# Turning blocks as whole sheets in a two-layer encoder on one core

## The chip, the cores and the metric

The kernel runs on one core of a Trainium2 chip. TensorE (PE in the profile) multiplies matrices, VectorE (DVE) and ScalarE (ACT) work on elements, and SyncE (SP) issues transfers on its own queue; GpSimd (POOL) makes only a few constants. Operands lie in SBUF, products are summed in PSUM, weights come from HBM. The metric is the device time of one execution in microseconds (us), here as the median of several runs.

## The reference

Two layers of an encoder over 256 rows (tokens) of width D = 2048, and 256 rows of memory. Everything is float32.

```python
h = rmsnorm(x, g);  proj = h @ w_in[l]                 # 2048 x 7168
a_x, a_b, a_c, a_g, d_q, d_k, d_v, d_g, m_q, m_g = split(proj)
# A: gated convolution over rows, 6 groups of 128 columns
y_a = a_b * conv3(a_c * a_x) * silu(a_g)
# D: differential attention, 6 heads of two halves of 64, q and k normed per half
y_d = silu(d_g) * (1 - lam_init) * rmsnorm((softmax(q1 k1 + alibi) - lam * softmax(q2 k2 + alibi)) v)
# M: attention of 4 heads of 128 into the memory, queries and keys normed
mk, mv = split(rmsnorm(mem) @ w_mem_kv[l])
y_m = silu(m_g) * softmax(norm(m_q) norm(mk)) mv
x = x + concat(y_a, y_d, y_m) @ w_out[l]
```

## The kernel before, in words

**Products and chunks.** The 256 rows are two row tiles of 128 (`NT`), the 2048 columns 16 k-tiles of 128 (`KT`). To keep float32 accuracy, each operand is split into a high and a low half, and each product is three matmuls: high by high (L250), high by low (L251), low by high (L252), each 128x128 by 128x512. `block` computes 512 columns of a projection for both row tiles in two PSUM accumulators. It walks the k-tiles in **chunks** of two (`CK`): one load of 512 KB into one of four raw buffers (L219, SyncE's queue), one high half by ScalarE (L225; with the gain of a norm L229), one low half by VectorE (L226, L230), four buffers of each, and 12 matmuls, 2.72 us at the spacing of the profile. There are 320 chunks, numbered here from 0: 0 to 7 the memory keys of layer 0, 8 to 15 its values, 16 to 23 the keys of layer 1 (x is loaded meanwhile, L581, eight transfers), 24 to 31 its values, 32 to 175 layer 0, 176 to 319 layer 1. In a layer come the six blocks of group D, the two of M, the six of A and the output projection (chunks 144 to 175 and 288 to 319).

**Turns.** The stationary operand of a product has the contracted columns on the partitions: it is a turned block, `xT`, `yT` and `memT`, as high and low half for each k-tile (`split_T`: high by ScalarE at L206 or L209, low by VectorE). Before the change there are three ways to turn a block of 256 rows by 512 columns:

- `turn`, for the memory heads' keys and queries: eight TensorE transposes of 128x128 (L337), evacuated by ScalarE with the gain (L340).
- `turn32`, for group D's queries and keys, the convolution's gate and input, and columns 0 to 1023 of layer 1's x: 16 VectorE transposes (L352), each of four partition quarters into one of four, in squares of 32x32. The squares are put in place by the instruction's own input and output, so each has 32 partitions.
- `x_rows` with `rows_T`, for all of layer 0's x and columns 1024 to 2047 of layer 1's: four TensorE transposes for two k-tiles (L518).

**What sets the order.** Such work is written as generators in the queue `side`; `run_side` takes one step after each chunk, and `later` holds a generator back for some chunks. A scheduler then orders the instructions of each engine by its own estimate of times and by their priority; `keep_in_program_order` pins some. What stands on an engine's queue behind an instruction that waits, waits too. Loads, halves and side work of one engine share its queue.

**Sums of squares.** `normed` squares both accumulators of a block (L315, ScalarE), sums by group (L316) and multiplies by the inverse root (L325). `x_square` sums the squares of x (L548): eight calls, for four column blocks and two row tiles, written before layer 0's first block.

Of the kernel before, what the change touches and what calls it, by code (L numbers as in the profile page):

```python
# [14 lines left out]
ALU = mybir.AluOpType  # L15
# [19 lines left out]
PARTS = 8  # L35

# [7 lines left out]
def encoder(ctx: ExitStack, tc: tile.TileContext, x, mem, norm_g, w_in, conv_w, conv_b,  # L44
# [83 lines left out]
    kgain = const.tile([P, DEPTH], F32, name="kgain")  # L128
    neglam = const.tile([P, DEPTH], F32, name="neglam")
    lam_init = [0.8 - 0.6 * math.exp(-0.3 * l) for l in range(DEPTH)]  # L130

    def rest_of_constants():
# [33 lines left out]
    side = deque()  # L166
# [3 lines left out]
    def later(g, n):  # L170

        due[id(g)] = chunk[0] + n
        return g

    def run_side(n=1, now=None):
        chunk[0] += now is None
        for _ in range(n):
            g = next((g for g in side if now or due.get(id(g), 0) <= chunk[0]), None)
            if g is None:
                return  # L180
            side.remove(g)
            try:
                next(g)
                if len(side) >= 1:
                    side.insert(1, g)
                else:
                    side.append(g)
            except StopIteration:
                due.pop(id(g), None)

    def flush_side():
        while side:
            run_side(now=True)
# [9 lines left out]
    def split_T(dst, k, src, gain):  # L203

        if gain is None:
            in_order(nc.scalar.copy(dst[:, 0, k, :], src),  # L206
                     nc.vector.tensor_tensor(dst[:, 1, k, :], src, dst[:, 0, k, :].bitcast(F32), ALU.subtract))
        else:
            nc.scalar.activation(dst[:, 0, k, :], src, AF.Copy, scale=gain)  # L209
            nc.vector.scalar_tensor_tensor(dst[:, 1, k, :], src, gain, dst[:, 0, k, :].bitcast(F32),  # L210
                                           ALU.mult, ALU.subtract)
# [22 lines left out]
    def block(stat, w, cols, order, steps=1, gain=None, before=None, apart=0, acc=None, more=False):  # L234
# [28 lines left out]
        for c in range(0, n, CK):  # L263
# [7 lines left out]
            for j in range(CK):  # L271
                k = k0 + j
                hi, lo = parts[j]
# [35 lines left out]
    def normed(acc, gs, st, whole=False):  # L309
# [10 lines left out]
        res = []  # L320
        both = tmp.tile([P, NT, NB], F32, tag="e", name=nm("nat")) if whole else None
        for t in range(NT):
            nc.vector.tensor_scalar(r[:, t], r[:, t], col(st, R, t), None, ALU.mult)
            y = both[:, t] if whole else tmp.tile([P, NB], F32, tag="nat", name=nm("nat"), bufs=4)
            nc.vector.tensor_tensor(y.rearrange("p (g d) -> p g d", d=gs),  # L325
                                    acc[t].rearrange("p (g d) -> p g d", d=gs),
                                    r[:, t].unsqueeze(2).to_broadcast([P, ng, gs]), ALU.mult)
            res.append(y)
        return both if whole else res

    def turn(nat, dests):


        for t in range(NT):
            pt = ps_t.tile([P, NB], F32, tag="t", name=nm("pt"))
            for j in range(NB // P):
                nc.tensor.transpose(pt[:, j * P:(j + 1) * P], nat[t][:, j * P:(j + 1) * P], ident)  # L337
            at = 0
            for dst, h0, nh, gain in dests:
                nc.scalar.activation(dst[:, h0:h0 + nh, t * P:(t + 1) * P],  # L340
                                     pt[:, at * P:(at + nh) * P].rearrange("p (h q) -> p h q", h=nh),
                                     AF.Copy, scale=gain)
                at += nh
            yield

    def turn32(dst, src):

        n = src.shape[-1] // P
        B = 32
        for b in range(P // B):  # L350
            for a in range(P // B):
                tc.keep_in_program_order(nc.vector.transpose(  # L352
                    dst[b * B:(b + 1) * B, 0:n].rearrange("p j (t a c) -> p t j a c", a=P // B, c=B)[:, :, :, a, :],
                    src[a * B:(a + 1) * B].rearrange("p t (j b c) -> p t j b c", b=P // B, c=B)[:, :, :, b, :]))
            yield
# [46 lines left out]
    def qk_T(l, yT, k2, nat, q, k, tag):  # L402

        whole = keep.tile([P, NB // P, SEQ], F32, tag=tag, name=nm("qk"))
        yield from turn32(whole, nat)
        if q is not None:
            c0, h0, nh = q
            a = c0 // P
            for c in range(2):
# [3 lines left out]
                nc.scalar.copy(hi, src)  # L413
                nc.vector.tensor_tensor(yT[other, c, h0:h0 + nh, :], src, hi.bitcast(F32), ALU.subtract)
                yield
        if k is not None:
            c0, h0, nh = k
            a = c0 // P
            for c in range(2):
# [4 lines left out]
                nc.scalar.activation(hi, src, AF.Copy, scale=g)  # L424
                nc.scalar.activation(yT[other, c, CG + h0:CG + h0 + nh, :], src, AF.Copy, scale=g)
                for at, n, dst, d0 in ((0, min(nh, 4 - h0), yT, CG + DH + h0), (4 - h0, h0 + nh - 4, k2, 0)):
                    if n > 0:
                        lo = dst[own, c, d0:d0 + n, :]
                        nc.vector.scalar_tensor_tensor(lo, whole[own, a + at:a + at + n, :], g,  # L429
                                                       hi[:, at:at + n].bitcast(F32), ALU.mult, ALU.subtract)  # L430
                        nc.scalar.copy(dst[other, c, d0:d0 + n, :], lo)
# [332 lines left out]
```

## Time and profile before

| | |
|---|---|
| median of three runs | 955.16 us (954.63 to 956.37) |
| the profiled execution | 953.96 us |
| its span, first to last instruction | 952.2 us |
| TensorE busy | 943.5 us, 99% |
| VectorE, ScalarE busy | 718.9 us (76%), 513.1 us (54%) |
| granted TensorE clock, mean | 0.999 |
| moved by transfers | 175.21 MB in 103,523 packets |

A row of groups reads: line, engine, operation, output and inputs, shape, count, then busy time, mean ns of one, and the idle time of the engine just before, with what ended it. A row of the timeline reads: start, duration, engine, line, operation, count of like neighbours that it joins, and in brackets the idle time before it. A row of waits reads: who waits, for what, microseconds in all, times, longest. Matmuls overlap: each takes about 0.39 us, and the next begins 0.23 us after it.

### The profile page before, as it was taken

The page shows a single profiled execution, that of the slowest core. Times are in us where ns is not written, and L with a number is a line of the kernel's source. Part 1 is how long each engine was busy: PE and PEld are TensorE (multiplying, and loading weights), DVE is VectorE, ACT ScalarE, POOL GpSimd, SP SyncE. Part 2 cuts the span into 40 slices and gives each one's busy share as a digit, 9 for nine tenths or more (in the row PEclk, how much of TensorE's full clock was granted, in tenths as well). Part 3 has the DMA queues.
Part 4 walks back from the last instruction along what each step waited for, and adds up shares of the span by engine and source line. Part 5 has one row for each costly group of instructions (what it writes and reads, how often), then busy time and mean ns, then how long its engine had stood idle before and what let it go on. Part 6 is the DMA issues. An engine that isn't in the chain of part 4 may idle for free.

```text
span 952.2 us, 12481 instructions
## 1 busy us (share of the span) xinstructions
PE 943.5 (99%) x4370; PEld 778.7 (82%) x4370; DVE 718.9 (76%) x1408; ACT 513.1 (54%) x803; POOL 1.4 (0%) x8
## 2 busy tenths in 40 slices
PE   8999999999999999999999999999999999999998
PEld 6888788888888888888878888888888888888886
DVE  5766679996677788668798679995677787569752
ACT  5857645675456654443555445675455645444531
POOL 0000000000000000000000000000000000000000
PEclk9999999999999999999999999999999999999999
DMA  8786556557655556654646666556665555654672
GB/s 269 258 267 193 159 180 191 168 164 226 187 169 162 168 159 181 183 161 131 227 147 226 191 186 196 160 172 221 177 177 164 168 159 173 181 173 155 196 251 83
DMA packets 103523, 175.21 MB, mean 184 GB/s; under 512 B 6318, under 2 KB 29732, under 8 KB 103460
## 3 DMA queue, kind: packets, MB, share of 16 engines
q1 hardware_dynamic: 102116, 173.09, 59.2%
q10 hardware_dynamic: 1344, 1.33, 0.5%
q8 instruction: 34, 0.56, 0.2%
q14 instruction: 29, 0.24, 0.1%
HBM read 172.29 MB, written 2.10 MB: 183 GB/s over the span
## 4 chain that ended last, share of the span: by engine, by line
PE 86%; DVE 10%; issue 2%; ACT 1%; DMA 0%; ACTq 0%; DVEq 0%
PE acc L251 27%; PE acc L252 27%; PE acc L250 26%; DVE lo L226 3%; PE po L382 2%; DVE uT L352 2%; DVE qk L352 1%; PE ptT L375 1%; DVE xf L352 1%; PE pt L518 1%; PE s L488 1%; ACT hi L225 1%; DVE yT L429 0%; DMA raw<-in_w_mem_kv_dram 0%; PE py L367 0%
## 5 line engine op out<-in xcount | busy, mean ns | idle before, releaser
L226 DVE TENSOR_TENSOR lo<-raw,hi 128x1024 fp32r<-128x1024 f32 x288 | 350.3, 1222 | 148.8 <-ACT hi L225 146.8
L225 ACT CAST hi<-raw 128x1024 fp32r<-128x1024 f32 x288 | 301.5, 1051 | 283.5 <-PE acc L252 234.6
L251 PE MATMUL acc<-lo,xT 128*128 128x512 f32 x896 | 352.0, 393 | 0.1
L252 PE MATMUL acc<-hi,xT 128*128 128x512 f32 x896 | 348.6, 392 | 0.0
L250 PE MATMUL acc<-hi,xT 128*128 128x512 f32 x896 | 348.4, 394 | 0.1
L251 PEld LDWEIGHTS acc<-lo,xT 128*128 128x128 f32 x896 | 168.4, 188 | 35.0 <-DVE lo L226 1.5
L250 PEld LDWEIGHTS acc<-hi,xT 128*128 128x128 f32 x896 | 168.4, 188 | 34.6 <-ACT xT L209 0.6
L252 PEld LDWEIGHTS acc<-hi,xT 128*128 128x128 f32 x896 | 167.9, 188 | 33.6
L251 PE MATMUL acc<-lo,yT 128*128 128x512 f32 x256 | 99.8, 391 | 2.0 <-DVE lo L226 2.0
L252 PE MATMUL acc<-hi,yT 128*128 128x512 f32 x256 | 98.0, 389 | 0.0
L250 PE MATMUL acc<-hi,yT 128*128 128x512 f32 x256 | 95.1, 390 | 0.0
L251 PEld LDWEIGHTS acc<-lo,yT 128*128 128x128 f32 x256 | 48.1, 188 | 13.6 <-DVE lo L226 3.7
L230 DVE SCALAR_TENSOR_TENSOR lo<-raw,cva,hi 128x512 fp32r<-128x512 f32 x64 | 45.6, 747 | 17.2 <-ACT hi L229 17.0
L250 PEld LDWEIGHTS acc<-hi,yT 128*128 128x128 f32 x256 | 48.1, 188 | 9.9
L252 PEld LDWEIGHTS acc<-hi,yT 128*128 128x128 f32 x256 | 48.1, 188 | 9.8
L229 ACT ACTIVATE hi<-raw,cva 128x512 fp32r<-128x512 f32 x64 | 42.5, 716 | 19.6 <-PE acc L252 14.9
L252 PE MATMUL acc<-hi,memT 128*128 128x512 f32 x124 | 48.6, 392 | 0.0
L251 PE MATMUL acc<-lo,memT 128*128 128x512 f32 x124 | 48.4, 390 | 0.0
L250 PE MATMUL acc<-hi,memT 128*128 128x512 f32 x124 | 44.4, 395 | 0.1
L352 DVE STREAM_TRANSPOSE qk<-nat 32x256 f32<-32x256 f32 x96 | 41.8, 436 | 1.5
L251 PEld LDWEIGHTS acc<-lo,memT 128*128 128x128 f32 x124 | 23.3, 188 | 5.0
L252 PEld LDWEIGHTS acc<-hi,memT 128*128 128x128 f32 x124 | 23.3, 188 | 4.9
(153 smaller groups left out, 725.5 us busy)
## 6 DMA issues: line engine op xcount, KB each, us to landing
raw<-in_w_in_dram SPq DMA_DIRECT2D x192, 512.0 KB
raw<-in_w_out_dram SPq DMA_DIRECT2D x64, 512.0 KB
raw<-in_w_in_dram SPq DMA_DIRECT2D x64, 256.0 KB
raw<-in_w_mem_kv_dram SPq DMA_DIRECT2D x31, 512.0 KB
xs<-in_x_dram SPq DMA_DIRECT2D x8, 256.0 KB
xs<-in_mem_dram SPq DMA_DIRECT2D x7, 256.0 KB
out_dram<-xs SPq DMA_DIRECT2D x8, 128.0 KB
out_dram<-xs ACTq DMA_DIRECT2D x8, 128.0 KB
```

The costliest lines, as they stand in the source:

```text
L225: nc.scalar.copy(hi, raw)
L226: nc.vector.tensor_tensor(lo_, raw, hi.bitcast(F32), ALU.subtract)
L229: in_order(nc.scalar.activation(hi[:, j], raw[:, j], AF.Copy, scale=gains_of(j)), nc.vector.scalar_tensor_tensor(lo_[:, j], raw[:, j], gai ...
L230: nc.vector.scalar_tensor_tensor(lo_[:, j], raw[:, j], gains_of(j), hi[:, j].bitcast(F32), ALU.mult, ALU.subtract))
L250: nc.tensor.matmul(acc[t], sh, hi, start=first, stop=False)
L251: nc.tensor.matmul(acc[t], sh, lo, start=False, stop=False)
L252: nc.tensor.matmul(acc[t], sl, hi, start=False, stop=last)
L352: tc.keep_in_program_order(nc.vector.transpose(dst[b * B:(b + 1) * B, 0:n].rearrange("p j (t a c) -> p t j a c", a=P // B, c=B)[:, :, :, a ...
L375: nc.tensor.transpose(pt[:, k, i * P:(i + 1) * P], e[:, i, k * P:(k + 1) * P], ident)
L382: nc.tensor.matmul(po[:, i, :], eT[:, k, i * P:(i + 1) * P], v[:, k, h * P:(h + 1) * P], start=k == 0, stop=k == NT - 1)
L488: nc.tensor.matmul(s[:, i, :], qT[:, h, i * P:(i + 1) * P], kT[:, h, :], start=True, stop=True)
L518: nc.tensor.transpose(pt[:, j, t * P:(t + 1) * P], src(k + j, t), ident)
```

## The change

**Sheets.** A block to be turned is written by its makers (`normed`, the gate, the convolution's products) straight into a **sheet**: 128 partitions by 4 column quarters by n groups by 2 row tiles by 32 columns. One VectorE transpose then turns every 32x32 square of the sheet where it lies (128 x 1024 values, or 512 for two groups); for x two transposes read `xs` and write the sheet. What is left is to move, for each of 16 pairs of partition quarters, a **strip** of 32 partitions, each with 8 pieces of 32 values (128 B), to its place in the turned tile. That is one transfer from SBUF to SBUF, 256 pieces, 32 KB, on SyncE's queue, 16 for a sheet. `run_side` releases up to seven strips after a chunk (`at_once`; five from layer 0's first block on), and the first strip comes `wait` chunks after the transpose (5; 4 for x; 3 once).

**Where.** All of `turn` and `turn32` go, and `x_rows` is left for one column block of layer 1's x: the memory heads' keys (two sheets) and queries (two), layer 0's x (four, turned while layer 1's memory keys and values are computed), three blocks of layer 1's x, and the blocks that `turn32` turned; 25 sheets, 400 strips. TensorE's transposes fall by 72 (32 of L337, 40 of the 80 of L518), VectorE's from 256 to 32.

**Beside it.** Turning work is kept in a list `tasks` of its own, of which every generator that is due takes a step after each chunk. The gains of memory queries and keys are multiplied together and applied once, to the keys (ScalarE, in place). In the convolution's part the blocks of C_X and C_C come in another order, and the whole scale of their product is put on the first.

```diff
-    def turn(nat, dests):
...
-    def turn32(dst, src):
...
+    def turn_sheet(dst, src, of=None, wait=5):
+        if of is None:
+            tc.keep_in_program_order(nc.vector.transpose(src, src))
+        else:
+            for t in range(NT):
                 tc.keep_in_program_order(nc.vector.transpose(
-                    dst[b * B:(b + 1) * B, 0:n].rearrange("p j (t a c) -> p t j a c", a=P // B, c=B)[:, :, :, a, :],
-                    src[a * B:(a + 1) * B].rearrange("p t (j b c) -> p t j b c", b=P // B, c=B)[:, :, :, b, :]))
-            yield
+                    src[:, :, :, t], of[:, t].rearrange("p (j b c) -> p b j c", b=NA, c=B)))
+        yield wait
+        left = [NA * NA]
+
+        def shift(a, b):
+            def go():
+                s, d = src[a * B:(a + 1) * B, b], dst[b * B:(b + 1) * B]
+                d = d.rearrange("p j (t a i) -> p (j t) a i", t=NT, a=NA)[:, :, a]
+                s = s.rearrange("p j t i -> p (j t) i")
+                tc.keep_in_program_order(nc.sync.dma_start(d, s))
+                left[0] -= 1
+            return go
+
+        for b in range(NA):
+            for a in range(NA):
+                shifts.append(shift(a, b))
+        while left[0]:
+            yield 1
...
+    def run_side(n=1, now=False):
+        chunk[0] += 1
+        for _ in range(len(shifts) if now else min(at_once[0], len(shifts))):
+            shifts.popleft()()
+        for g in list(tasks):
+            if now or due.get(id(g), 0) <= chunk[0]:
+                step(g, tasks)
         for _ in range(n):
...
+    def keys(l, nat):
+        yield from turn_sheet(mkT[l], nat)
+        tc.keep_in_program_order(nc.scalar.activation(mkT[l], mkT[l], AF.Copy, scale=mgain[:, l:l + 1]))
...
     def x_load(k):
...
+        b, half = divmod(k + 2, NB // P)
+        if not half:
+            tasks.append(later(x_turned(xT, 0, b - 1, ("v", "ga", "mga", "mqT")[b - 1], wait=4), 1))
...
         if l > 0:
-            side.append(turn(normed(acc_k, P, stm[0]), [(mkT[l], 0, MH, cvb[:, 56 + l:57 + l])]))
-            xT = T_tile("xT")
-            side.append(x_rows(xT, 0, range(0, KT, 2)))
+            tasks.append(later(keys(l, normed(acc_k, P, stm[0], sheets("e"))), 12))
...
             if l + 1 < DEPTH:
-                side.append(later(x_turned(xT, l + 1, b, ("mga", "ga")[b]), 3) if b < 2 else
-                            x_rows(xT, l + 1, range(4 * b, 4 * b + 4, 2)))
+                if b < 3:
+                    tasks.append(later(x_turned(xT, l + 1, b, ("mga", "ga", "v")[b], wait=4), 4))
+                else:
+                    side.append(later(x_rows(xT, l + 1, range(4 * b, 4 * b + 4, 2)), 2))
```

How the order moves is shown at three places. In the rows stand line, operation, output, inputs and shape; lines of the two kernels differ (L219 becomes L249, L225 L255, L226 L256, L229 L259, L315 L347, L548 L608, L209 L238).

ScalarE around the change from layer 1's memory keys to its values, before. `hi` are high halves of chunks 23 (`hi_117`) and on, `sq` from `acc` the squares of the keys:

```order
L229 ACTIVATE hi_117_798<-raw_116_796,cva_114 128x512 x2
L229 ACTIVATE hi_130_849<-raw_129_847,cva_114 128x512 x2
L229 ACTIVATE hi_135_884<-raw_134_882,cva_114 128x512 x2
L229 ACTIVATE hi_140_919<-raw_139_917,cva_114 128x512 x2
L315 ACTIVATE sq_120_817<-acc_93_646 128x512
L315 ACTIVATE sq_121_821<-acc_94_647 128x512
L229 ACTIVATE hi_144_948<-raw_143_946,cva_114 128x512 x2
L229 ACTIVATE hi_149_986<-raw_148_984,cva_114 128x512 x2
```

The same place after; `hi_121` is chunk 23, `hi_134` chunk 24, `hi_137` chunk 25, and `sq` from `xs` are squares of x:

```order
L259 ACTIVATE hi_121_809<-raw_120_807,cva_114 128x512 x2
L259 ACTIVATE hi_134_869<-raw_133_867,cva_114 128x512 x2
L238 ACTIVATE xT_90_634<-xf_99_681,cvb_118 128x256 x2
L347 ACTIVATE sq_126_839<-acc_91_637 128x512
L347 ACTIVATE sq_127_843<-acc_92_638 128x512
L608 ACTIVATE sq_157_1106,ssx_123<-xs_92 128x512
L608 ACTIVATE sq_158_1108,ssx_123<-xs_92 128x512
L608 ACTIVATE sq_159_1110,ssx_123<-xs_92 128x512
L608 ACTIVATE sq_160_1112,ssx_123<-xs_92 128x512
L259 ACTIVATE hi_137_900<-raw_136_898,cva_114 128x512 x2
L238 ACTIVATE xT_90_634<-xf_99_681,cvb_118 128x256 x2
```

Before, the squares of the keys stand behind the high half of chunk 26; after, behind that of chunk 24, with pieces of x's turn and four squares of x beside them, and four more squares of x behind the last row shown.

SyncE's queue at the same place, before (`raw_116` is chunk 23's load):

```order
L219 DMA raw_113_775<-in_w_mem_kv_dram 128x2x512
L581 DMA xs_92<-in_x_dram 128x2x256
L219 DMA raw_116_796<-in_w_mem_kv_dram 128x2x512
L219 DMA raw_129_847<-in_w_mem_kv_dram 128x2x512
L219 DMA raw_134_882<-in_w_mem_kv_dram 128x2x512
```

After (`raw_120` is chunk 23's, `xf` a turned block of x, `mkT0` the turned keys of layer 0, L396 the strips):

```order
L249 DMA raw_120_807<-in_w_mem_kv_dram 128x2x512
L396 DMA xf_99_681<-sh_100_682 32x8x32 x7
L646 DMA xs_92<-in_x_dram 128x2x256
L396 DMA xf_99_681<-sh_100_682 32x8x32 x7
L249 DMA raw_133_867<-in_w_mem_kv_dram 128x2x512
L396 DMA xf_99_681<-sh_100_682 32x8x32 x2
L396 DMA mkT0_126<-sh_80_567 32x8x32 x5
L249 DMA raw_136_898<-in_w_mem_kv_dram 128x2x512
L396 DMA mkT0_126<-sh_80_567 32x8x32 x7
L249 DMA raw_139_929<-in_w_mem_kv_dram 128x2x512
```

Fourteen strips and a load of x come between the loads of chunks 23 and 24, and seven between each two loads that follow, for 80 strips in all.

VectorE in layer 0's output projection, before (`xs` is the new x of a block, `xf` its turned block):

```order
L724 TENSOR_TENSOR xs<-acc_4071,xs 128x512
L724 TENSOR_TENSOR xs<-acc_4072,xs 128x512
L352 STREAM_TRANSPOSE xf_4414<-xs 32x2x4x32 x8
L226 TENSOR_TENSOR lo_4452<-raw_4449,hi_4451 128x1024
L352 STREAM_TRANSPOSE xf_4414<-xs 32x2x4x32 x4
L724 TENSOR_TENSOR xs<-acc_4187,xs 128x512
L226 TENSOR_TENSOR lo_4474<-raw_4471,hi_4473 128x1024
```

After:

```order
L808 TENSOR_TENSOR xs<-acc_4105,xs 128x512
L808 TENSOR_TENSOR xs<-acc_4106,xs 128x512
L256 TENSOR_TENSOR lo_4490<-raw_4487,hi_4489 128x1024
L386 STREAM_TRANSPOSE sh_4506<-xs 128x16x32 x2
L256 TENSOR_TENSOR lo_4512<-raw_4509,hi_4511 128x1024
L256 TENSOR_TENSOR lo_4530<-raw_4527,hi_4529 128x1024
```

Sixteen transposes between low halves become two.

More of the change, by code (lines that the diff above doesn't have):

```diff
@@ L173, in later, with step @@
         return g
-    def run_side(n=1, now=None):
-        chunk[0] += now is None
+    def step(g, where, at=None):
+        where.remove(g)
+        try:
+            due[id(g)] = chunk[0] + (next(g) or 1)
+        except StopIteration:
+            due.pop(id(g), None)
+            return
+        if at is not None and len(where) >= at:
+            where.insert(at, g)
+        else:
+            where.append(g)
+    def run_side(n=1, now=False):
[5 more added lines that the diff above has]
+                step(g, tasks)
         for _ in range(n):
@@ L180, in run_side, with flush_side, settle @@
                 return
[L181 to L192, printed above, removed]
+            step(g, side, 1)
+    def flush_side(what=None):
+        what = side if what is None else what
+        while what:
+            run_side(now=True)
+    made = set()
+    kept = []
+    def settle(stat, k):
+        while (id(stat), k) not in made:
+            assert side or tasks
+            print("forced", chunk[0], k)
             run_side(now=True)
@@ L329, in normed @@
-        return both if whole else res
-    def turn(nat, dests):
[L334 to L343, printed above, removed]
-            yield
@@ L404, in qk_T @@
         whole = keep.tile([P, NB // P, SEQ], F32, tag=tag, name=nm("qk"))
-        yield from turn32(whole, nat)
+        yield from turn_sheet(whole, nat)
+        pin = tc.keep_in_program_order
         if q is not None:
@@ L635, in encoder, with turn_mq @@
         acc = block(xT, w_in[l], [(C_M, NB)], ALLK)
-        nat = normed(acc, P, st)
-        side.appendleft(turn(nat, [(mqT, 0, MH, cvb[:, 54 + l:55 + l])]))
+        def turn_mq(nat):
+            yield from turn_sheet(mqT, nat)
+            queries.add(l)
+        tasks.append(later(turn_mq(normed(acc, P, st, sheets("bgx"))), 8))
         acc = block(xT, w_in[l], [(C_M + W_MEM, NB)], ALLK)
@@ L678, in conv, with both_rows, scaled, times @@
                 nc.vector.tensor_tensor(yT[:, 1, g, :], z, yT[:, 0, g, :].bitcast(F32), ALU.subtract)
+                made.add((id(yT), g))
                 yield
+        def both_rows(dst, j0, j1):
+            return [by_columns(dst[:, :, j0:j1, t]) for t in range(NT)]
+        def scaled(dst, acc, by):
+            for t in range(NT):
+                nc.scalar.activation(dst[t], columns(acc[t]), AF.Copy, scale=col(st, by, t))
+        def times(dst, acc):
+            for t in range(NT):
+                nc.vector.tensor_tensor(dst[t], columns(acc[t]), dst[t], ALU.mult)
@@ L706, in encoder @@
+        scaled(both_rows(ux, 0, 4), acc, R2)
+        acc = block(xT, w_in[l], [(C_C, NB)], ALLK)
+        times(both_rows(ux, 0, 4), acc)
+        tasks.append(later(conv([0, 1, 2, 3], ux), 6))
+        acc = block(xT, w_in[l], [(C_X + NB, 256), (C_C + NB, 256)], ALLK)
+        scaled(both_rows(ux, 4, 6), [a[:, 0:256] for a in acc], R2)
+        times(both_rows(ux, 4, 6), [a[:, 256:512] for a in acc])
+        tasks.append(later(conv([4, 5], ux, wait=3), 4))
         flush_side()
-        side.append(conv([0, 1, 2, 3], ux))
```

151 lines of the change are left out of this document (84 added, 67 removed).

## The prediction

> **What bounds the kernel now.** I read the page first (busy shares, the chain by engine), then the waits of TensorE and of SyncE's queue, the groups by shape, and the timelines around TensorE's gaps.
>
> ```profile
> PE 943.5 (99%) x4370; PEld 778.7 (82%) x4370; DVE 718.9 (76%) x1408; ACT 513.1 (54%) x803; POOL 1.4 (0%) x8
> PE 86%; DVE 10%; issue 2%; ACT 1%; DMA 0%; ACTq 0%; DVEq 0%
> PE acc L251 <- DVE lo L226: 2.0, 4, 1.1
> SPq L219 <- DVE lo L226: 438.6, 178, 8.0
> ```
>
> TensorE is busy 99% of 952.2 us and its chain holds 86%. Its longest kind of wait is 2.0 us, four times, for a low half `lo` that VectorE made late. Weight loads wait 438.6 us for a raw buffer that VectorE has not yet emptied: they run as far ahead as four buffers allow, and memory does not bound. So time can come from three places only: instructions that leave TensorE's queue, gaps that vanish, and gaps that appear.
>
> **The transposes that leave TensorE.** The change takes out all 32 of L337 and 40 of the 80 of L518 (32 for layer 0's x, 8 for layer 1's block 2); 72 in all. Their price is read in the row of products:
>
> ```profile
> L518 PE MATMUL pt<-ident,xs 128*128 128x128 f32 x80 | 12.2, 277 | 1.0 <-DMA xs<-in_mem_dram 0.6 <-DVE lo L230 0.2
> L337 PE MATMUL pt<-ident,nat 128*128 128x128 f32 x32 | 4.6, 272 | 0.0
> 62.59 0.39 PE L251 MATMUL acc<-lo,memT 128*128 128x512 f32 x1
> 62.81 1.03 PE L337 MATMUL pt<-ident,nat 128*128 128x128 f32 x8
> 63.60 0.48 PE L252 MATMUL acc<-hi,memT 128*128 128x512 f32 x1
> 63.92 0.39 PE L250 MATMUL acc<-hi,memT 128*128 128x512 f32 x1
> ```
>
> Products start 0.22 to 0.23 us apart (62.59, 62.81). Without the eight transposes L252 would stand at 62.81 and L250 at 63.04; L250 stands at 63.92. Eight cost 0.88 us, 0.11 each, less than half of their duration because they overlap. 72 x 0.11 = **-8.0 us**. The trace has no other work that could have filled these slots, so this gain is not hidden. The Trainium skill, "TensorE: Matmul & The Clock Gate", Part 4, gives about 275 ns for a transpose in a kernel's context; the row's 272 to 277 agree as a duration, and priced so the 72 would be worth 19.8 us. Spacing, not duration, is what the queue loses, so I keep 0.11.
>
> **The gaps that vanish.** In the body the turns by VectorE are 16 instructions to a sheet, and low halves stand behind them:
>
> ```profile
> L352 DVE STREAM_TRANSPOSE qk<-nat 32x256 f32<-32x256 f32 x96 | 41.8, 436 | 1.5
> L352 DVE STREAM_TRANSPOSE bgT<-bg 32x128 f32<-32x128 f32 x32 | 9.7, 302 | 0.5
> 492.33 3.56 DVE L352 STREAM_TRANSPOSE xf<-xs 32x256 f32<-32x256 f32 x8
> 495.93 2.36 DVE L226 TENSOR_TENSOR lo<-raw,hi 128x1024 fp32r<-128x1024 f32 x2
> 495.50 0.61 PE L250 MATMUL acc<-hi,yT 128*128 128x512 f32 x2
> 497.21 0.50 PE L251 MATMUL acc<-lo,yT 128*128 128x512 f32 x1 [1.09 <-DVE lo L226]
> 497.55 0.40 PE L252 MATMUL acc<-hi,yT 128*128 128x512 f32 x1
> 486.70 0.61 PE L250 MATMUL acc<-hi,yT 128*128 128x512 f32 x2
> 488.00 0.39 PE L252 MATMUL acc<-hi,yT 128*128 128x512 f32 x1
> 448.05 1.07 PE L250 MATMUL acc<-hi,yT 128*128 128x512 f32 x4
> 449.73 0.39 PE L252 MATMUL acc<-hi,yT 128*128 128x512 f32 x1
> 207.92 0.61 PE L250 MATMUL acc<-hi,xT 128*128 128x512 f32 x2
> 208.92 0.40 PE L252 MATMUL acc<-hi,xT 128*128 128x512 f32 x1
> ```
>
> From 495.50 to 497.55 there are three spacings, 0.68 us, in 2.05 us: 1.37 lost, right behind eight transposes of 3.56 us. In the same way 486.70 to 488.00 loses 0.62 (three spacings), 448.05 to 449.73 0.54 (five) and 207.92 to 208.92 0.32 (three). The first three are three of the four waits of 2.0 us in all; the fourth, in layer 1, is the like of 448.05 and worth the same 0.54. That is 3.4 us. Gaps like the last, too short to be called waits, stand at a few more places; I put them at 0.7 in all and take 4.1. The change leaves one or two transposes to a sheet. Their price is extrapolated from 302 ns at 128 columns and 436 at 256: 168 ns + 1.05 ns a column gives 0.70 us for 512 columns and 1.24 for 1024, if 128 partitions cost as 32 do. The bounds are one 32x256 instruction (0.44) and the whole old sheet (16 x 0.436 = 7.0); I take 1.24, since both rows differ in columns alone. VectorE's sheet falls from 7.0 to about 1.3 us, the order gives every weight chunk of the body three chunks of lead, and the gaps go: **-4.1 us** (bounds 0 and -4.5).
>
> **What the strips cost.** 25 sheets leave 16 transfers each, 400 on SyncE's queue, 23 full sheets' worth: 23 x 4,096 = 94,208 packets of 128 B. No transfer within SBUF and none of this packet size stands in the trace. The nearest rows:
>
> ```profile
> q1 hardware_dynamic: 102116, 173.09, 59.2%
> q10 hardware_dynamic: 1344, 1.33, 0.5%
> 43.03 0.37 SPq L219 DMA_DIRECT2D raw<-in_w_mem_kv_dram  x1
> 43.45 0.46 SPq L581 DMA_DIRECT2D xs<-in_x_dram  x1
> ```
>
> A packet takes 0.592 x 952.2 x 16 / 102,116 = 88 ns at 1,695 B on q1, and 57 ns at 990 B on q10. A line through both gives 18 ns at 128 B; in proportion to bytes it would be 7, at q10's whole price 57. I take 18: a transfer of 256 packets over 16 engines is 0.29 us of each (0.91 at 57 ns). All together 94,208 x 18 / 16 = 106 us, 11% of the span, on top of 59%: the body has room, and waits at least four chunks (4 x 2.72 = 10.9 us) between a sheet's last strip and its reader. So the body pays nothing; at 57 ns the total would be 94% and the body would pay. The Trainium skill, "DMA: Bandwidth & Descriptors", Specifications, puts line rate at 512 B and more and names read-modify-write below; its section "Why small descriptors are slow (HBM only)" exempts SBUF to SBUF. No run here shows either yet; the first rule works against this change.
>
> **The head (chunks 24 to 34) is where the change can lose.** Two things move there. First ScalarE's order: two squares of layer 1's keys, which wait for the last product of chunk 23, and four squares of x now stand ahead of the high half of chunk 25, four more ahead of chunk 26's. Before, halves of three further chunks stood ahead of the squares.
>
> ```profile
> 77.06 1.28 ACT L315 ACTIVATE sq<-acc 128x512 f32<-128x512 f32 x2 [0.70 <-PE acc L252]
> 77.55 0.39 PE L250 MATMUL acc<-hi,memT 128*128 128x512 f32 x1
> L548 ACT ACTIVATE sq<-xs 128x512 f32<-128x512 f32 x16 | 9.9, 622 | 1.2 <-DVE xs L724 1.2
> L548 ACT ACTIVATION_READ_ACCUMULATOR sq<-xs 128x1 f32 x16 | 3.0, 186 | 0.0
> L209 ACT ACTIVATE xT<-xf,cvb 128x256 fp32r<-128x256 f32 x8 | 3.4, 498 | 1.9 <-DVE xf L352 1.9
> L229 ACT ACTIVATE hi<-raw,cva 128x512 fp32r<-128x512 f32 x64 | 42.5, 716 | 19.6 <-PE acc L252 14.9
> L230 DVE SCALAR_TENSOR_TENSOR lo<-raw,cva,hi 128x512 fp32r<-128x512 f32 x64 | 45.6, 747 | 17.2 <-ACT hi L229 17.0
> L599 ACT ACTIVATE mv<-acc,stm 128x512 f32<-128x512 f32 x4 | 2.7, 689 | 1.2 <-PE acc L252 1.2
> ```
>
> Chunk 24 starts at 77.55, 0.88 earlier after the change: 76.67, and the squares at 76.18. They end at 77.46; four squares of x at 0.62 + 0.19 = 0.81 end at 80.70; the high half of chunk 25 at 81.42, its low half at 82.17. TensorE wants it at 76.67 + 2.72 + 0.23 = 79.62: 2.55 lost. Then the second high half (82.13), two pieces of x at 0.50 (83.13), four squares (86.37), the halves of chunk 26 (87.84), wanted at 84.89: 2.95 lost. Chunk 27 comes in time. At chunk 33 two evacuations of 0.69 stand ahead; I put 0.9. Sum **+6.4 us**, with bounds 0 (if the x squares found earlier idle time, which a fixed order excludes) and about 9.
>
> Second, SyncE's queue: up to seven strips stand between two weight loads, for eight loads in a row.
>
> ```profile
> 57.54 17.33 SPq L219 DMA_DIRECT2D raw<-in_w_mem_kv_dram  x7
> 1.22 0.47 ACTq L219 DMA_DIRECT2D raw<-in_w_mem_kv_dram  x1
> 5.49 1.34 ACT L229 ACTIVATE hi<-raw,cva 128x512 fp32r<-128x512 f32 x2 [1.10 <-DMA raw<-in_w_mem_kv_dram]
> L225 ACT CAST hi<-raw 128x1024 fp32r<-128x1024 f32 x288 | 301.5, 1051 | 283.5 <-PE acc L252 234.6
> L226 DVE TENSOR_TENSOR lo<-raw,hi 128x1024 fp32r<-128x1024 f32 x288 | 350.3, 1222 | 148.8 <-ACT hi L225 146.8
> ```
>
> The first of those seven loads (57.54) is chunk 23's. Behind it come 14 strips and a load of x: 15 x 0.45 us, so chunk 24's load goes at about 64 to 65. From there a load costs one period P: by issue 7 x 0.45 + 0.37 = 3.5 us; by DMA work 1.7 (512 KB are 309 packets of 1,695 B, at 88 ns over 16 engines) + 7 x 0.29 = 3.7; and if each load must find its predecessor landed, about the 4 us from 1.22 to 5.49. I take 3.8, bounds 3.2 (0.40 to issue) and 8.1 (57 ns). Chunk 32's load then goes at 65 + 8P, its low half is there 3.8 + 1.05 + 1.22 us later, and TensorE wants it at 76.67 + 8 x 2.72 + 0.23 = 98.66. The delay is 8P - 27.6: 2.8 at 3.8, hidden in the 5.5 already lost to ScalarE; it passes 6.4 at P = 4.25. So nothing is added.
>
> **Sum.** 953.96 (the profiled execution: span 952.2 and 1.8 around it) - 8.0 - 4.1 + 6.4 = 948.3. The median of the runs is 1.2 above the profiled time: **949.5 us**.
>
> **Rivals.** (1) The strips pace the head: P above 5.25 us, that is a strip above 0.69 us to issue or above 32 ns a packet. The delay 8P - 27.6 replaces the 6.4: at P = 6 it is 20.4, and 953.96 - 12.1 + 20.4 + 1.2 = 963.5; at 57 ns (P = 8.1) 980 and more in the body. For it speaks that no row has such a packet and q10's small ones are dearer per byte; against it, 18 ns is far below 32. The skill's rule for transfers below 512 B would act as this. 16%. (2) New waits in the body take the place of the old (a strip late for its reader, ScalarE behind it): the 4.1 come back, 953.6, or a little more. 12%. (3) The gaps of 2.55 and 2.95 us cost the clock as well. The longest gap in the trace is 1.1 us and the granted clock 0.999, so nothing shows it; if one chunk of 12 products after each runs at half rate, 2 x 2.72 = 5.4 are added, 954.9. The Trainium skill, "TensorE: Matmul & The Clock Gate", "Why this matters for your kernels", names gaps above about 3 us; by it both just escape. 6%. (4) The head's gaps are smaller than I reckon, 0 to 2 us: 943 to 945. 10%. Forecast: 56%.
>
> **How the numbers follow.** 0.2% (1.9 us) is about what a measurement of this kernel can tell from no change: faster below 953.25, slower above 957.07. Faster gets the forecast, rival 4 and a few points of 2 and 3: 0.70; same the rest of these: 0.14; slower rival 1: 0.16. The range 943 to 957 holds the forecast (own range 946 to 952) and rivals 2, 3 and 4, and P up to 5.2.
>
> **What would show it.** Right: no L337, 40 of L518 left; no wait for `lo` above 0.3 us between 110 us and the end; two gaps of two to three us at chunks 25 and 26 with ScalarE on squares of x before them; SyncE's strips 0.4 to 0.5 us apart, a mean packet of the whole below 60 ns, DMA share near 70%. Wrong: TensorE waiting for a DMA behind chunk 28, a strip above 0.7 us, or a clock below 1 in the head.

## The result, and the profile after

The change makes the kernel slower: **964.47 us** (963.86 to 964.75) against 954.89 (954.23 to 956.37) before it, a ratio of 1.0097 with a 95% interval of 1.008 to 1.0115. Forecast were 949.5, with a range up to 957. The profiled execution took 964.53 us, its span is 962.7. Of the four runs of four_128b, one of the experiments below, one took 1,039.02 us at a granted clock of 0.851 (0.996 to 0.997 in the other three, whose median is 948.26), and its ratio leaves that run out.

The page of the changed kernel: engines, granted clock in 40 slices of 24 us, packets, queue, chain.

```profile
PE 943.5 (98%) x4298; PEld 777.1 (81%) x4298; DVE 647.5 (67%) x1188; ACT 509.0 (53%) x797; POOL 1.4 (0%) x8
PE   9997699999999999999999999999999999999998
PEclk9998999999999999999999999999999999999999
DMA packets 204133, 187.30 MB, mean 195 GB/s; under 512 B 106926, under 2 KB 130340, under 8 KB 204068
q1 hardware_dynamic: 202724, 185.17, 66.7%
PE 94%; DMA 2%; SPq 2%; ACT 1%; DVE 0%; issue 0%; DVEq 0%; ACTq 0%
```

VectorE is busy 71 us less than before. TensorE is idle in the fourth and fifth slice, 72 to 120 us, and hardly anywhere else (7 and 6 in the row of tenths); the granted clock falls in the fourth (8). The waits of TensorE say for what:

```profile
PE acc L280 <- ACT hi L259: 7.6, 4, 2.5
PE acc L281 <- DVE lo L260: 2.5, 3, 1.5
```

These are halves of weights, late. ScalarE's timeline says why (the high halves of chunks 24 to 27; the first waited 6.87 us for its load):

```profile
75.03 1.34 ACT L259 ACTIVATE hi<-raw,cva 128x512 fp32r<-128x512 f32 x2 [6.87 <-DMA raw<-in_w_mem_kv_dram]
80.71 1.32 ACT L259 ACTIVATE hi<-raw,cva 128x512 fp32r<-128x512 f32 x2
86.53 1.34 ACT L259 ACTIVATE hi<-raw,cva 128x512 fp32r<-128x512 f32 x2 [1.25 <-DMA raw<-in_w_mem_kv_dram]
91.74 1.33 ACT L259 ACTIVATE hi<-raw,cva 128x512 fp32r<-128x512 f32 x2 [2.84 <-DMA raw<-in_w_mem_kv_dram]
```

SyncE's queue says why the loads are late (the duration of a joined row is its whole stretch):

```profile
61.08 4.66 SPq L396 DMA_DIRECT2D xf<-sh  x7
65.84 0.55 SPq L646 DMA_DIRECT2D xs<-in_x_dram  x1
66.43 4.51 SPq L396 DMA_DIRECT2D xf<-sh  x7
71.04 0.55 SPq L249 DMA_DIRECT2D raw<-in_w_mem_kv_dram  x1
...
108.75 4.53 SPq L396 DMA_DIRECT2D xf<-sh  x7
113.39 0.55 SPq L249 DMA_DIRECT2D raw<-in_w_in_dram  x1
```

Seven strips take 4.5 us of the queue, 0.64 each, though each moves only 32 KB, and the queue issues without a break from 61.08 to 113.39: chunk 24's load goes at 71.04, chunk 32's at 113.39, one in (113.39 - 71.04) / 8 = 5.29 us, while TensorE uses a chunk up in 2.72. Chunk 32 starts there:

```profile
118.84 0.78 PE L280 MATMUL acc<-hi,xT 128*128 128x512 f32 x2 [2.02 <-ACT hi L255]
```

Before the change its first product stood here:

```profile
100.69 0.39 PE L250 MATMUL acc<-hi,xT 128*128 128x512 f32 x1
```

So the head lost 18.15 us, and the rest of the program (962.7 - 118.84 = 843.9 against 952.2 - 100.69 = 851.5) gained 7.6. Their sum is the 10.5 us between the two spans.

### The profile page after: what moved, and what is told of

Same layout as the page of the kernel before. It is cut to its first block, busy times and chain, and to the rows that moved or that the text cites. A ratio compares the mean times of both kernels' runs of the same rounds, so it can differ in the third digit from the quotient of the medians.

```text
span 962.7 us, 12648 instructions
## 1 busy us (share of the span) xinstructions
PE 943.5 (98%) x4298; PEld 777.1 (81%) x4298; DVE 647.5 (67%) x1188; ACT 509.0 (53%) x797; POOL 1.4 (0%) x8
## 4 chain that ended last, share of the span: by engine, by line
PE 94%; DMA 2%; SPq 2%; ACT 1%; DVE 0%; issue 0%; DVEq 0%; ACTq 0%
PE acc L282 29%; PE acc L281 29%; PE acc L280 29%; PE po L431 2%; SPq L396 1%; PE ptT L424 1%; DMA raw<-in_w_mem_kv_dram 1%; PE s L543 1%; PE s L493 1%; PE s L492 1%; PE pt L573 1%; ACT sq L608 1%; DMA raw<-in_w_in_dram 0%; PE py L416 0%; DMA xs<-in_mem_dram 0%; ACT hi L259 0%
## 5 line engine op out<-in xcount | busy, mean ns | idle before, releaser
L256 DVE TENSOR_TENSOR lo<-raw,hi 128x1024 fp32r<-128x1024 f32 x288 | 351.7, 1224 | 216.7 <-ACT hi L255 214.0
L255 ACT CAST hi<-raw 128x1024 fp32r<-128x1024 f32 x288 | 302.3, 1051 | 331.8 <-PE acc L282 271.8
L280 PE MATMUL acc<-hi,xT 128*128 128x512 f32 x896 | 352.9, 396 | 2.4 <-ACT hi L255 2.4
L282 PE MATMUL acc<-hi,xT 128*128 128x512 f32 x896 | 351.3, 392 | 0.0
L282 PE MATMUL acc<-hi,yT 128*128 128x512 f32 x256 | 99.6, 389 | 0.0
L280 PE MATMUL acc<-hi,yT 128*128 128x512 f32 x256 | 99.1, 389 | 0.0
L259 ACT ACTIVATE hi<-raw,cva 128x512 fp32r<-128x512 f32 x64 | 42.4, 716 | 35.1 <-DMA raw<-in_w_mem_kv_dram 24.4
L281 PE MATMUL acc<-lo,memT 128*128 128x512 f32 x124 | 51.0, 412 | 2.6 <-DVE lo L260 2.5
L280 PEld LDWEIGHTS acc<-hi,memT 128*128 128x128 f32 x124 | 23.4, 195 | 14.4 <-ACT hi L259 9.3
L282 PEld LDWEIGHTS acc<-hi,memT 128*128 128x128 f32 x124 | 24.4, 197 | 5.1
```

The lines of the kernel that those rows point to most:

```text
L255: nc.scalar.copy(hi, raw)
L256: nc.vector.tensor_tensor(lo_, raw, hi.bitcast(F32), ALU.subtract)
L259: in_order(nc.scalar.activation(hi[:, j], raw[:, j], AF.Copy, scale=gains_of(j)), nc.vector.scalar_tensor_tensor(lo_[:, j], raw[:, j], gai ...
L280: nc.tensor.matmul(acc[t], sh, hi, start=first, stop=False)
L281: nc.tensor.matmul(acc[t], sh, lo, start=False, stop=False)
L282: nc.tensor.matmul(acc[t], sl, hi, start=False, stop=last)
```

## The experiments

**Theory Q**: the strips cost SyncE's queue, by the transfer and not by the byte, and the weight loads stand behind them. **Rival S**: ScalarE's order, squares of x ahead of the halves of chunks 25 and 26 (the prediction's own term). **Rival D**: the packets of 128 B occupy the DMA engines. The first four runs tell them apart.

**x0_rows: layer 0's x back on TensorE.**

```diff
     def x_load(k):
-        b, half = divmod(k + 2, NB // P)
-        if not half:
-            tasks.append(later(x_turned(xT, 0, b - 1, ("v", "ga", "mga", "mqT")[b - 1], wait=4), 1))
...
+            side.append(x_rows(xT, 0, range(0, KT, 2)))
...
+                    steps=1 if l == 0 else 2)
```

> The changed kernel, but layer 0's x is turned by TensorE again (32 transposes at 0.11 us come back, 64 of the 80 strips of the head go). Theory Q (the strips' issue on SyncE's queue, 0.64 us each, delays the loads of chunks 24 to 32): the 22 us lost in the head go to about 1 to 2, TensorE pays 3.6 again: 946 us. Rival S (ScalarE's order, squares of x before the halves of chunks 25 and 26): the squares are still eight among the halves of chunks 26 to 29, so several us of loss should stay: 950 or more. Rival D (the packets of 128 B themselves occupy the DMA engines): as Q.

Measured: 944.31 us (943.92 to 944.64), ratio 0.9889 (0.9874 to 0.9904). Chunk 32 starts at 100.99, and these are all of TensorE's waits:

```profile
PE warm L114 <- DVE zeros L109: 1.2, 1, 1.2
PE pt L573 <- DMA xs<-in_mem_dram: 0.7, 1, 0.7
```

The head's loss is gone, and so is the body's of before (2.0 us of waits for `lo`). What remains of the change makes the kernel 1.1% faster than before it; only the strips of layer 0's x made it slower. Its squares of x still stand among the halves, of chunks 27 to 30, and cost nothing, against S.

**sq_early: ScalarE's order alone.** Six of the eight squares of x are issued while x is loaded.

```diff
         if not half:
+            if b > 1:
+                for t in range(NT):
+                    x_square(b - 2, t)
             tasks.append(later(x_turned(xT, 0, b - 1, ("v", "ga", "mga", "mqT")[b - 1], wait=4), 1))
...
-    for c in range(4):
-        for t in range(NT):
-            x_square(c, t)
+    for t in range(NT):
+        x_square(3, t)
```

> The changed kernel, but six of the eight squares of x are issued while x is being loaded, so that they stand ahead of chunk 24's high half by six chunks; SyncE's order stays word for word. Q: the loads stay late, so at most 1 to 2 us are won: 962 to 964.5. Rival S: the two gaps at chunks 25 and 26 go, 5.5 us and the slow clock behind them (about 6 us): 953 to 958.

Measured: 967.14 us (966.08 to 967.93), ratio 1.0126 (1.0109 to 1.0143): nothing won, some 2.7 lost against the changed kernel. Chunk 24's load goes at 72.04, a microsecond later than there. With the squares out of the way, chunk 26's high half still waits 4.18 us for its load, and the products 2.97 us for that half. S is not what made the change slow.

**four_128b: the same packets in a quarter of the transfers.**

```diff
+        def quarter(b):
+            def go():
+                d = dst.rearrange("p j (t a i) -> p (j t) a i", t=NT, a=NA)[:, :, b]
+                s = src[:, b].rearrange("p j t i -> p (j t) i")
+                tc.keep_in_program_order(nc.sync.dma_start(d, s))
+                left[0] -= NA
+            return go
+
         for b in range(NA):
-            for a in range(NA):
-                shifts.append(shift(a, b))
+            if at_once[0] == 7 and of is not None:
+                shifts.append(quarter(b))
+            else:
+                for a in range(NA):
+                    shifts.append(shift(a, b))
```

> The changed kernel, but for layer 0's x each four strips are one transfer of 128 partitions, 1,024 pieces of 128 B: the same packets and bytes in a quarter of the transfers (16 instead of 64). The pieces are not put in their places, so layer 0's x is wrongly turned. Q with a price per transfer: issue about 0.6 us each, the head's loss falls to below 3 us: 943 to 947. Q with a price per packet: issue about 2.4 us each, the loss stays: 960 to 964. Rival D: the packets are the same, the loss stays: 960 to 964, with a high DMA share in the head.

Measured: 948.44 us, ratio 0.993 (0.9914 to 0.9947), a little above the 943 to 947 that a price per transfer was to give. The row of these transfers (least, median and longest ns), from the answer for their line:

```profile
L404 SPq DMA_DIRECT2D xf<-sh x16: 594/680/1887, 61.1 to 90.6; - x16
```

The stretch of the head, with the busy time of each engine, the granted clock, the DMA share and GB/s at the end:

```profile
58.00:95.00 37.00, 32.79 (x136) 26.21 (x135) 29.39 (x67) 24.38 (x51) 0.00 (x0) 0.91 0.82 187
```

A transfer of 1,024 pieces takes 0.68 us to issue in the median, one of 256 takes 0.61 (the median of 608 ns in the changed kernel). With the longest of them (1.89) all 16 take 14.0 us of the queue, 0.88 each, where 64 strips at 0.64 take 41. So the price is in the main the transfer's. The same number of bytes and packets of x cost the head 5.5 us in place of 18, against D. (By count of products chunk 32 begins at about 106.2; its first products, at 103.97, stand ahead of ten of chunk 31's.) The DMA engines do more in the same time (share 0.82); of the changed kernel the same view gives, for its stretch of strips:

```profile
61.00:113.00 52.00, 42.37 (x158) 31.89 (x157) 29.88 (x76) 25.82 (x51) 0.00 (x0) 0.90 0.58 130
```

Its DMA engines stood at 0.58, 130 GB/s: the queue could not hand them the work.

**pool_head: the head's strips on GpSimd's queue.**

```diff
-                tc.keep_in_program_order(nc.sync.dma_start(d, s))
+                tc.keep_in_program_order((nc.gpsimd if at_once[0] == 7 else nc.sync).dma_start(d, s))
```

> The changed kernel, but the head's 80 strips go on GpSimd's queue instead of SyncE's; GpSimd has nothing else to do there. The packets are the same. Q: the loads of chunks 24 to 32 go as before the change, the head's loss falls to below 3 us: 942 to 946, unless GpSimd's own issue is so slow (over 1 us a strip) that layer 0's x comes late, which would show as TensorE waiting for xT at chunk 32. Rival D: the loss stays, 960 to 964.

Measured: 961.19 us (957.45 to 962.37), ratio 1.0059 (1.0036 to 1.0082). The expectation's exception came true at a lower price than it named. The loads go on time, by SyncE's timeline:

```profile
58.01 22.63 SPq L249 DMA_DIRECT2D raw<-in_w_mem_kv_dram  x9
```

The strips are late, by the answer for their line and TensorE's waits:

```profile
L396 POOL DMA_DIRECT2D xf<-sh x64: 582/582/722, 61.0 to 119.8; - x64
```

```profile
PE acc L280 <- DVE sh L356: 4.4, 1, 4.4
PE acc L280 <- ACT xT L238: 3.1, 2, 1.5
```

Nine loads in 22.6 us, chunk 32 at 99.17, sooner than before. But GpSimd pays 0.58 us a strip too; the last strip of x is issued at about 120 us, and TensorE waits four times for `xT`, from 105 to 120.5 us. So the queue changes who is late, not the price: 80 transfers of 0.58 us are 47 us of some queue, in a stretch of 59. The price is not all of the loss here. In 13 of the 59 us GpSimd's queue stands still, in half of them for the third sheet's transposes:

```profile
100.21 7.05 POOL L396 DMA_DIRECT2D xf<-sh  x12 [6.32 <-DVE sh L386]
```

After x, 15 strips of layer 1's keys stand on SyncE's queue ahead of a load (122.44 to 132.34), and at 161 us TensorE waits 4.4 us for an accumulator that VectorE empties into a sheet (`sh`, L356); why that comes so late was not followed up.

**head_halves: the same packets in twice the transfers.** One run.

```diff
-                tc.keep_in_program_order(nc.sync.dma_start(d, s))
+                for h in ((0, B // 2), (B // 2, B)) if at_once[0] == 7 else ((0, B),):
+                    tc.keep_in_program_order(nc.sync.dma_start(d[h[0]:h[1]], s[h[0]:h[1]]))
```

> The changed kernel, but each of the head's strips is two transfers of 16 partitions, 128 pieces each: the same packets in twice the transfers (160 instead of 80). Q with a price per transfer: a period of 14 x 0.6 + 0.55 = 9 us, chunk 24's load 9 us later, so about 40 us more than the changed kernel: 995 to 1010. Q with a price per packet, or rival D (DMA engines): 962 to 967.

Measured: 1017.31 us, above the forecast of 995 to 1010.

```profile
72.30 8.94 SPq L397 DMA_DIRECT2D xf<-sh  x14
81.33 0.54 SPq L249 DMA_DIRECT2D raw<-in_w_mem_kv_dram  x1
```

```profile
L397 SPq DMA_DIRECT2D xf<-sh x176: 585/598/745, 62.5 to 593.6; - x176
```

The first fence is SyncE's timeline, the second the answer for the strips' line (its 176 take in 48 whole strips of layer 1). Half a strip (128 pieces) takes as long to issue as a whole one, 0.60 against 0.61, and 14 take 8.94 us, 0.64 each. Chunk 24's load goes at 81.33, and the kernel is 53 us slower than with 80 transfers. Price by the transfer, from 128 to 1,024 pieces.

**x_early4 and x_early7: strips spread over more chunks, four or seven at once.** Both keep all of the change; they differ in one number.

```diff
-    at_once = [7]
+    at_once = [4]
...
-            tasks.append(later(keys(0, normed(acc_k, P, stm[0], sheets("e"))), 6))
+            tasks.append(later(keys(0, normed(acc_k, P, stm[0], sheets("bgT"))), 25))
...
-            tasks.append(later(x_turned(xT, 0, b - 1, ("v", "ga", "mga", "mqT")[b - 1], wait=4), 1))
+            tasks.append(later(x_turned(xT, 0, b - 1, ("v", "ga", "mga", "mqT")[b - 1], wait=1), 1))
...
-            tasks.append(later(keys(l, normed(acc_k, P, stm[0], sheets("e"))), 12))
+            tasks.append(later(keys(l, normed(acc_k, P, stm[0], sheets("bgx"))), 18))
```

> All of the change kept, layer 0's x by strips too, but the strips are spread: the first sheet's strips follow one chunk after its transpose (four before), at most four strips between two loads (seven before), and the memory keys' two sheets wait in other buffers until x is through. Theory Q (0.61 us of SyncE's queue a strip): a period is 4 x 0.61 + 0.55 = 3.0 us for 16 loads, 4.5 us over what TensorE needs, which the lead of the loads covers; the head loses less than 2 us and TensorE saves the 32 transposes of x: 940 to 942.5. Rival: what is lost in the head hangs on the count of strips, 64 to 80, or on their packets, wherever they stand: 950 and more.

> As the kernel that spreads the strips of layer 0's x over more chunks, but with seven at once instead of four. Same strips, same packets, same early start. Q: a period of 7 x 0.61 + 0.55 = 4.8 to 5.2 us for nine loads in a row, some 20 us over need, of which the lead of the loads covers about 10: 5 to 12 us lost, 947 to 955. Rival (only the late start mattered): as with four, 940 to 943.

Measured: with four 949.21 us (948.66 to 949.52), ratio 0.9941 (0.9928 to 0.9953); with seven 961.98 (960.47 to 962.38), ratio 1.0072 (1.0058 to 1.0086). The same 64 strips of x are worth 12.8 us by how many stand between two loads: against the rival that only their count mattered. But four did not reach 942.5, and seven came out 7 us past the upper end: its 21 strips and three loads of x stand together ahead of chunk 22's load already (53.44 to 69.67 us of SyncE's timeline), earlier than I had reckoned. Four at once, SyncE's queue:

```profile
84.41 0.55 SPq L249 DMA_DIRECT2D raw<-in_w_mem_kv_dram  x1
85.00 2.55 SPq L396 DMA_DIRECT2D xf<-sh  x4
87.65 0.55 SPq L249 DMA_DIRECT2D raw<-in_w_mem_kv_dram  x1
```

and TensorE:

```profile
83.59 0.73 PE L280 MATMUL acc<-hi,memT 128*128 128x512 f32 x2 [0.87 <-ACT hi L259]
84.78 0.50 PE L281 MATMUL acc<-lo,memT 128*128 128x512 f32 x1 [0.46 <-DVE lo L260]
88.07 0.73 PE L280 MATMUL acc<-hi,memT 128*128 128x512 f32 x2 [0.72 <-ACT hi L259]
89.69 0.50 PE L281 MATMUL acc<-lo,memT 128*128 128x512 f32 x1 [0.89 <-DVE lo L260]
```

A load goes every 3.24 us, still more than 2.72, so the halves' lead melts, and two gaps of 1.3 and 1.6 us open where ScalarE has squares of x before the halves. Whether the loads or the squares set those gaps, the next run asks.

**x_early4s: four at once, and the squares of x early** (the edits of x_early4 and of sq_early together).

> As the kernel that spreads layer 0's x's strips four at a time, and six of the eight squares of x issued while x is loaded. Theory: with loads of one in 3.25 us, ScalarE's squares of x decide at chunks 27 and 28 (the gaps of 0.87 + 0.46 and 0.72 + 0.89 us in the run without this edit stand behind them); moved away, 2 to 3 us are won: 946 to 947.5. If the loads alone paced it: 949, no gain.

Measured: 948.30 us (947.00 to 950.36), ratio 0.9933 (0.992 to 0.9945). 0.9 less at the median, with overlapping spreads: not told from no gain, and below the 2 to 3 forecast. The trace shows where the gain went. The two gaps are gone: TensorE's waits name no half of chunks 16 to 31, and chunk 28 comes nearly 4 us sooner after chunk 16 than without the edit. But chunk 36 comes only about 1.2 us sooner after it, and the edit has a wait of its own, 1.03 us at 56.70, where TensorE waits for ScalarE to empty an accumulator (`mv`). So the squares set where the gaps stood, and the loads most of what is lost in all.

**x_half3: a period below TensorE's.** The edits of x_early4 with three at once, and only the first half of x by strips.

```diff
-    at_once = [7]
+    at_once = [3]
...
-        if not half:
+        if not half and b <= 2:
...
+            side.append(x_rows(xT, 0, range(KT // 2, KT, 2)))
```

> Only the first half of layer 0's x by strips, early and three at a time between loads, the second half by 16 TensorE transposes; the rest of the change kept. Theory: a period of 3 x 0.61 + 0.55 = 2.4 us is below the 2.72 us that TensorE takes for a chunk, so no load is late, and 16 transposes less than with all of x on TensorE save 1.8 us of the 944.3: 942 to 943.5. If any strip in the head costs (buffers, DMA): 945 to 948.

Measured: 943.55 us (943.47 to 943.96), ratio 0.9883 (0.9868 to 0.9898), the fastest of all. Three strips and a load take 2.57 us on SyncE's queue, and TensorE's waits, which follow it, hold none for a weight:

```profile
72.44 0.53 SPq L249 DMA_DIRECT2D raw<-in_w_mem_kv_dram  x1
73.02 1.89 SPq L396 DMA_DIRECT2D xf<-sh  x3
75.01 0.55 SPq L249 DMA_DIRECT2D raw<-in_w_mem_kv_dram  x1
```

```profile
PE pt L573 <- DMA xs<-in_mem_dram: 1.3, 2, 0.9
PE warm L114 <- DVE zeros L109: 1.2, 1, 1.2
```

It is 0.8 us below x0_rows, not the 1.8 of 16 transposes; the first product of chunk 32 stands at 100.96 here and at 100.99 there. The two were not timed side by side, so no more is made of it.

**body_16: how much room the body has.** x0_rows, with all 16 strips of a sheet between two loads from layer 0 on.

```diff
-            at_once[0] = 5
+            at_once[0] = 16
```

> The kernel with layer 0's x on TensorE, but all 16 strips of a sheet between two loads in the body, instead of five. Q: 16 x 0.61 = 9.8 us without a load, while four raw buffers hold loads for about 8 to 11 us: 0 to 1.5 us lost at each of some 18 sheets, 945 to 965. If the lead of the loads in the body is larger than that, 944 to 945.

Measured: 966.94 us (963.44 to 968.71), ratio 1.0125 (1.0102 to 1.0148): 22.6 us slower than with five at once. In the projections most sheets pass; around the output projections they do not. SyncE's queue, a sheet that passed and one that did not:

```profile
166.15 10.85 SPq L396 DMA_DIRECT2D qk<-sh  x16
...
439.41 13.08 SPq L396 DMA_DIRECT2D uT<-sh  x16
452.58 21.68 SPq L249 DMA_DIRECT2D raw<-in_w_out_dram  x12
```

```profile
458.16 0.73 PE L280 MATMUL acc<-hi,yT 128*128 128x512 f32 x2 [2.15 <-ACT hi L255]
```

The second fence is TensorE behind the latter. The lead of the loads covered 10.85 us without one, and 13.08 not. "The body pays nothing" holds for five at once, not for the strips as such.

All runs against before, with the first product of chunk 32 and what lies from there to the span's end:

| kernel | median us | ratio | chunk 32 at | rest of span |
|---|---|---|---|---|
| before | 954.9 to 955.3 | | 100.69 | 851.5 |
| the change | 964.47 | 1.0097 | 118.84 | 843.9 |
| sq_early | 967.14 | 1.0126 | 120.34 | 845.3 |
| x_early7 | 961.98 | 1.0072 | 118.56 | 842.0 |
| pool_head | 961.19 | 1.0059 | 99.17 | 861.4 |
| head_halves | 1017.31 | one run | 165.03 | 850.5 |
| body_16 | 966.94 | 1.0125 | 100.35 | 863.3 |
| x_early4 | 949.21 | 0.9941 | 102.97 | 844.7 |
| four_128b (x not put in place) | 948.44 | 0.993 | 103.97 | 842.5 |
| x_early4s | 948.30 | 0.9933 | 103.10 | 842.9 |
| x0_rows | 944.31 | 0.9889 | 100.99 | 841.6 |
| x_half3 | 943.55 | 0.9883 | 100.96 | 840.4 |

In four_128b ten products of chunk 31 stand behind this first product, in x_early7 four: counted by products, chunk 32 begins there at about 106.2 and 119.5.

## Why the prediction was wrong, step by step

**The transposes, -8.0: right.** The time that runs of other TensorE work take out of the row of products falls from 55.5 us before to 47.6 (worked out from the trace, product by product), 7.9 less. In x0_rows, which has 32 of them again, it is 50.7, 4.8 less for 40 transposes: 0.12 each. The duration of 0.27 us, which the Trainium skill ("TensorE: Matmul & The Clock Gate", Part 4) gives too, would have forecast 19.8.

**The gaps that vanish, -4.1: right.** From 125 us to the end (before: the same chunks) the products' own row loses 4.6 us less than before, and no wait for `lo` is left behind 126 us. (Three of about 0.5 us stand at 114.22, 120.10 and 125.56, where none above 0.3 was forecast; they belong to the late loads of the head.) The price of a sheet was met too: 1.24 and 0.70 us were extrapolated from rows of 32 partitions.

```profile
L383 DVE STREAM_TRANSPOSE sh<-sh 128x1024 f32<-128x1024 f32 x14 | 17.3, 1236 | 0.0
L386 DVE STREAM_TRANSPOSE sh<-xs 128x512 f32<-128x512 f32 x14 | 9.2, 690 | 8.1 <-DMA mkT<-sh 6.4 <-DMA xf<-sh 1.7
```

**The packets: right in what follows, and cheaper than taken.** q1's time rose from 0.592 x 952.2 to 0.667 x 962.7 us of 16 engines, 78.4 us for 100,608 more packets: 12.5 ns a packet against 18 taken (bounds 7 and 57). Of these, 94,208 are the forecast packets of 128 B and 6,400 are packets of 4 B, 16 to a strip; by the trace's own records of packets they take 13.0 and 9 ns. The Trainium skill, "DMA: Bandwidth & Descriptors", "Why small descriptors are slow (HBM only)", says transfers within SBUF are spared. The trace agrees only in part: a byte in these packets takes 0.10 ns of an engine, in the loads' packets 0.05 (88 ns for 1,695 B). Whether the read-modify-write that the same page of the Trainium skill names under Specifications had a share in that, no run here shows.

**The head, SyncE's queue: here the prediction failed.** Two terms. First, "by issue 7 x 0.45 + 0.37 = 3.5 us": 0.45 was read from rows of loads of x (0.46), as if a transfer of 32 KB cost no more than those. Measured: 0.61 to issue, 0.64 from one to the next, and 0.55 for a load that stands among strips, so P is 5.29, not 3.8. The bounds of 3.2 and 8.1 held it, but the upper end came from the DMA engines, and the value was taken near the lower. Second, "chunk 24's load goes at about 64 to 65" was priced at the same 0.45 and then kept fixed, in the rival too, when P was varied: 14 strips and a load of x took it to 71.04. With both measured values the prediction's own formula gives 71.04 + 8 x 5.29 + 6.1 - 98.66 = 20.8 us of delay; measured are 19.6 at the first product, and half a microsecond more at the first low half. Chunk 24 began here:

```profile
77.50 0.62 PE L280 MATMUL acc<-hi,memT 128*128 128x512 f32 x2
```

Eight chunks of 2.72 us from there end at 99.26, and chunk 32 began at 118.84. (The 0.88 us that chunk 24 was to come earlier does not show, 77.50 against 77.55: in this execution chunk 4 already began 0.9 later than before, at 21.96 against 21.05. x0_rows and body_16, whose edits differ only from layer 0 on, have 21.73 and 21.11 there, so single executions differ by that much.) The mechanism, its place and its form were right, as rival 1; its price and so its chance of 16% were not. Rival 1 asked for P above 5.25 and 963.5 at P = 6; it came at 5.29 since the start was late as well.

**The head, ScalarE's order, +6.4: not shown.** Gaps stand at chunks 25 and 26, but the loads set nearly all of them: chunk 24's load landed 4.0 us after its issue (71.04 to 75.03), chunk 25's by that at 80.2, and the squares held its half until 80.71, half a microsecond. Chunk 26's half waits 1.25 us for its load with the squares done. sq_early and x_early4s won nothing that can be told. Where the loads are in time the order is another, and nothing is lost to the squares: in pool_head five stand ahead of the half of chunk 28 and three ahead of that of chunk 29, and no product waits for a half there. Why the scheduler orders them so, no run shows.

**Rival 3, the clock: it happened, and decided little.** Behind some of the gaps the products stand 0.43 us apart in place of 0.23:

```profile
87.30 0.73 PE L280 MATMUL acc<-hi,memT 128*128 128x512 f32 x2 [2.07 <-ACT hi L259]
89.53 0.80 PE L281 MATMUL acc<-lo,memT 128*128 128x512 f32 x1 [1.49 <-DVE lo L260]
90.12 0.63 PE L282 MATMUL acc<-hi,memT 128*128 128x512 f32 x1
90.55 0.63 PE L281 MATMUL acc<-lo,memT 128*128 128x512 f32 x1
...
102.48 0.74 PE L280 MATMUL acc<-hi,memT 128*128 128x512 f32 x2 [1.93 <-ACT hi L259]
104.30 0.63 PE L280 MATMUL acc<-hi,memT 128*128 128x512 f32 x2
108.33 0.73 PE L280 MATMUL acc<-hi,memT 128*128 128x512 f32 x2 [2.48 <-ACT hi L259]
110.97 1.05 PE L280 MATMUL acc<-hi,memT 128*128 128x512 f32 x2
```

(Two joined products take 0.63 us at the full rate, 1.05 at the slow one.) At the slow rate a chunk takes 12 x 0.43 = 5.1 us, just what the loads allowed (5.29), and SyncE's queue did not stand still for it: its stretch from 61 to 113 us has no pause. So the slow clock cost little beyond the waiting; how much exactly, no run here separates.

**The signs that the prediction named** served: strips 0.64 us apart where 0.4 to 0.5 was to be right (0.7 was named as wrong, too far off), and a clock below 1 in the head. No L337 and 40 of L518's transposes were left, as named, and q1's share was near 70%; waits for `lo` above 0.3 us behind 110 us came all the same. "TensorE waiting for a DMA" showed as a wait for ScalarE's half, with the DMA one step further back.

## What to carry to other kernels

Price a transfer on its queue, not only in the DMA engines: here each strip cost some 0.6 us of issue, four strips in one 0.7 to 0.9, half a strip no less than a whole one, and what stands behind it on that queue is late by the sum. Compare the period between two loads, strips included, with the time in which the engines use a load up: 2.57 us against 2.72 was free, 3.24 cost several microseconds over 14 loads, 5.29 with a late start cost about 19. And when a bound of a rival is varied, vary every term that has the same price in it, the start of the stretch among them.

## What the runs showed of the hardware

- Issue by the transfer, medians: 0.60 us for 16 partitions and 128 pieces of 128 B, 0.61 for 32 and 256, 0.68 for 128 and 1,024 (0.88 on average), on SyncE's queue; 0.58 for 32 and 256 on GpSimd's. A load of 512 KB took 0.37 alone and 0.55 among strips.
- Packets of 128 B within SBUF took 13.0 ns of a DMA engine each, by the records of the 94,208 of them; packets of 4 B took 9 ns.
- The granted clock fell to about half after idle time of 2.48 us (at 108.33) and of 2.07 + 1.49 close together, and not after 1.93 us (at 102.48). The length of the gaps does not decide alone: in pool_head the clock was 0.51 from 108 to 115 us, behind gaps of 1.54 and 1.24 us, and 1.00 from 118 to 125, among gaps of 1.54 and 1.25. The Trainium skill, "TensorE: Matmul & The Clock Gate", "Why this matters for your kernels", warns of gaps above about 3 us; here shorter ones sufficed.
